# Conditioning loads issued from GpSimd's queue instead of SyncE's, in a two-layer backbone block

## The chip, the cores and the metric

The kernel runs on one core of one Trainium2 chip. The metric is the device time of one execution in microseconds, the median of several runs. Beside the times there is one profiled execution, from whose trace the rows below are read.

## What is computed

A latent stream of 256 tokens with 2048 channels goes through two layers. Layer 0 mixes tokens with a bidirectional gated recurrence and a spatial gating, layer 1 with a grouped two-dimensional Fourier transform; each mixer is followed by an MLP with a squared ReLU (2048 to 8192 to 2048). Every sublayer is wrapped in a norm, and shift, scale and gate of each norm come from a conditioning vector c through one large matrix per layer. That last part is what the change touches:

```python
for l in range(DEPTH):
    g_pre_m, g_post_m, g_pre_f, g_post_f = norm_gain[l]
    mx = [m[:, None, :] for m in jnp.split(jax.nn.silu(c) @ w_ada[l] + b_ada[l], N_MOD, axis=-1)]
    ...
    hx = modulate(x, g_pre_m, mx[0], mx[1])
    ...
    x = x + mx[2] * rmsnorm(mix_x, g_post_m)
    x = x + mx[5] * rmsnorm(sq_relu_mlp(modulate(x, g_pre_f, mx[3], mx[4]), w_mlp_in[l], w_mlp_out[l]), g_post_f)
...
def sq_relu_mlp(h, w1, w2):
    return jnp.square(jax.nn.relu(h @ w1)) @ w2
```

w_ada is 2 x 2048 x 12288 in float32, b_ada 2 x 12288. Twelve chunks of 2048 columns result, six for each layer; ten of them are "deferred" in the kernel and worked off beside the weight products.

## The kernel before

All weights stream once from HBM, as loads of [128, 2048] float32 (1 MB each, class Weights, L148) into raw tiles: two buffers `wr`, and while `spare` is set every second load goes to `ar` instead. A load holds two units of [128, 1024]. Each unit is split into a rounded high part `wh` by ScalarE (L70) and a rest `wl` by VectorE (L71), four buffers each, and TensorE makes three products of each pair (L67) instead of one. `W.get()` splits up to three units ahead of the one that TensorE is at.

The deferred conditioning (class Ada) works chunk by chunk, 16 steps a chunk. A step loads 1 MB of w_ada into one of the two `ar` buffers (L298) and adds it, times one value of silu(c), to `acc` on VectorE: the first step is a plain scaling (L301), the other 15 are multiply-adds (L307). For a gate chunk (columns 2 and 5) the first step also loads a bias row into an `ar` buffer (L304) and adds it (L305). A finished chunk is summed over the partitions by TensorE; for a gate, a row of norm gains is loaded to all partitions, also into `ar` (L351). There is one `acc` buffer, so a chunk's first step waits until the chunk before has been read.

`pump` hands out steps in the program's text: after each weight unit, 0.45 of a step in the mixer of layer 0, 0.36 in the MLP of layer 0 (which works off chunks (0,5), (1,0), (1,1), (1,3), (1,2) and begins (1,4)), 0.6 in the mixer of layer 1, 0.09 behind it; chunk (1,5) falls into the MLP of layer 1. The text's order is not the final one: the tile framework schedules the program by its own model of durations, and the instructions of each engine and each queue then stand in a fixed order and are taken in that order. What a queue's next instruction waits for holds up everything behind it on that queue.

Before the change every load, weights and conditioning, is issued by SyncE. GpSimd only prepares constants at the start.

Of the kernel before, what the change touches and what calls it, by code (L numbers as in the profile page):

```python
# [15 lines left out]
P = 128  # L16
D = 2048
KT = 16
# [18 lines left out]
def block_kernel(ctx: ExitStack, tc: tile.TileContext, a: dict, out: bass.AP, taps=None):  # L37
# [13 lines left out]

    # activations: quads of four [P, 512] slabs, and two single slabs
    def quad(dt=F32R):
# [7 lines left out]
    def slabs(n):  # L61
        """n slabs out of new quads."""
        qs = [quad() for _ in range((n + 3) // 4)]
        return [qs[i // 4][:, i % 4] for i in range(n)]
# [56 lines left out]
    class Weights:  # L121
        """Weights stream in program order: 1 MB loads, split by halves into hi + lo parts ahead of their use."""
        AHEAD = 3
# [58 lines left out]
        def place(self, u, at):  # L182
            """Unit u goes to four [P, 512] tiles: hi, hi, lo, lo."""
            assert u >= self.split_at
            self.places[u] = at
# [9 lines left out]
    class Background:  # L195
        """Latency-bound work, handed out in steps between the weight products."""

# [22 lines left out]

    # constants and small vectors
    ident = cp.tile([P, P], F32, name="ident")
# [20 lines left out]

    # silu of the conditioning vectors
    sc = cp.tile([P, 2, KT], F32, name="sc")
# [20 lines left out]
    def rstd_m2(ss, n):  # L266
        """-2 / sqrt(ss / n + eps), for the chains between sublayers."""
        s = sm.tile([P, 1], F32, name="rs")
        nc.scalar.activation(s, ss, AF.Sqrt, bias=epsb, scale=1.0 / n)
        v = sm.tile([P, 1], F32, name="rv")  # L270
        nc.vector.tensor_scalar(v, ss, 1.0 / n, EPS, ALU.mult, ALU.add)
        r = sm.tile([P, 1], F32, name="rr")
        nc.vector.reciprocal(r, s)
        e = sm.tile([P, 1], F32, name="re")
        nc.vector.scalar_tensor_tensor(e, r, r, v, ALU.mult, ALU.mult)
        r2 = sm.tile([P, 1], F32, name="rr2")
        nc.vector.scalar_tensor_tensor(r2, e, 3.0, r, ALU.subtract, ALU.mult)
        return r2

    # deferred adaLN chunks: products on VectorE, sums over partitions on TensorE  # L280
    class Ada:
# [11 lines left out]
        def step(self):  # L293
            l, c = self.order[self.pos]
            k = self.kt
            cols = slice(c * D, (c + 1) * D)
            raw = ap_.tile([P, D], F32, name="ar", tag="ar")
            nc.sync.dma_start(raw, a["w_ada"][l, k * P:(k + 1) * P, cols])  # L298
            if k == 0:
                self.acc = ap_.tile([P, D], F32, name="acc", tag="acc", bufs=1)  # L300
                self.queued(lambda: nc.vector.tensor_scalar_mul(self.acc, raw, sc[:, 0, 0:1]))  # L301
                if c in (2, 5):
                    brow = ap_.tile([P, D], F32, name="ar", tag="ar")
                    nc.sync.dma_start(brow[0:1, :], a["b_ada"][l:l + 1, cols])  # L304
                    nc.vector.tensor_add(self.acc[0:1, :], self.acc[0:1, :], brow[0:1, :])  # L305
            else:
                self.queued(lambda: nc.vector.scalar_tensor_tensor(self.acc, raw, sc[:, 0, k:k + 1], self.acc,  # L307
                                                                   ALU.mult, ALU.add))
            self.kt += 1
            if self.kt == KT:  # L310
                self.kt = 0
                self.pos += 1
                self.hold = 3
                if c in (2, 5):
                    self.done[(l, c)] = self.acc
                    if (l, c) != (0, 2):
                        self.hold = 8
                        bg.add(new_gate(l, c))
                else:
                    r = cp.tile([P, KT], F32, name=f"mod_{l}_{c}")  # L320
                    self.done[(l, c)] = r
                    bg.add(self.finish_cols(l, c, self.acc, r), front=True)
# [23 lines left out]
        def gate(self, l, c, dst):  # L346
            """-0.5 * gate * gain over all partitions (the factor meets rstd_m2)."""
            acc = self.done[(l, c)]
            gb = ap_.tile([P, D], F32, name="ar", tag="ar")
            row = l * 4 + (1 if c == 2 else 3)  # L350
            nc.sync.dma_start(gb, a["gain_rows"][row:row + 1, :].broadcast_to([P, D]))  # L351
            yield
            for b in range(4):
                t = ps()
                s = slice(b * 512, (b + 1) * 512)
                hi = rp.tile([P, 512], F32R, name="ghi", tag="xs")
                lo = rp.tile([P, 512], F32R, name="glo", tag="hh")
                split(hi, lo, acc[:, s])
                mm(t, ones_r, hi, True, False)
                mm(t, ones_r, lo, False, True)  # L360
                nc.vector.scalar_tensor_tensor(dst[:, s], t, -0.5, gb[:, s], ALU.mult, ALU.mult)
                yield
# [23 lines left out]

# [1 line left out]
    sp = tc.tile_pool(name="startp", bufs=1)  # L388
# [4 lines left out]
    def norms():  # L393
        """1 / rms of all tokens, over all partitions."""
        ss = ps()
# [18 lines left out]

    # lower bounds: softmax over the layers, first entry
    lb = cp.tile([P, 2, 8], F32, name="lb")
# [92 lines left out]
    def mm3(o, whi, wlo, h, start, stop):  # L509
        """Weights stationary: h holds hi | lo over T tokens."""  # L510
        mm(o, whi, h[:, 0:T], start, False)
        mm(o, whi, h[:, T:2 * T], False, False)
        mm(o, wlo, h[:, 0:T], False, stop)

    def tk3(o, h, t, whi, wlo, start, stop):
        """Tokens stationary: h holds hi | lo over T tokens; t picks the token tile."""
        hh = h[:, t * P:(t + 1) * P]
        hl = h[:, T + t * P:T + (t + 1) * P]
        mm(o, hh, whi, start, False)
        mm(o, hh, wlo, False, False)  # L520
        mm(o, hl, whi, False, stop)
# [39 lines left out]

# [1 line left out]
    gpool_cm = tc.tile_pool(name="gla", bufs=1)  # L563
# [9 lines left out]
    def proj_T(oL, oC, startL=True):  # L573
        """Weights stationary: one 128-column block, transposed output."""
        for half in range(2):
# [118 lines left out]
    def gla(p, st):  # L694
# [26 lines left out]

        # states left by the context
        Kt = gt("Kt", 1)
# [60 lines left out]
    def grow(Ff, Fb, KF, KB, QF, QB, B, keep):  # L784
        """Decay products over blocks of B become products over blocks of 2B."""
        n = 512 // (2 * B)
# [21 lines left out]

    # spatial gating
    vt = [[None, None], [None, None]]  # L810
# [65 lines left out]

# [1 line left out]
    rp = ctx.enter_context(tc.tile_pool(name="rp", bufs=2))  # L878
# [20 lines left out]
    def evac_product(t, nb, b, gate):  # L899
        """y <- gate * product, with the sum of squares of the product first."""  # L900
        square_sum(b, ssp[t][:, nb:nb + 1])
        yield
        nc.vector.tensor_mul(y[t][nb], gate[:, nb * 512:(nb + 1) * 512], b)
# [11 lines left out]
    def last_block(lhs, banks, start):  # L915
        """The last units of a product: the first token tile is finished before the second."""
        units = [W.get(LEAD - 1 - i) for i in range(LEAD)]
# [5 lines left out]
    def tokens_product(lhs, key, spare, upto, early=None, late=None):  # L923
        """y[t, :] = sum over KT blocks, tokens stationary."""
        gate = gates[key]
# [32 lines left out]
    def residual(evac, next_mods, consume):  # L958
        """x += gate * rmsnorm(product); next sublayer's modulated input, transposed, hi | lo.

        consume(h, t, nb) issues the next sublayer's work on token tile t, channel blocks 4 nb .. 4 nb + 3."""
        h = None
# [6 lines left out]
        def scale(parts):  # L969
            """-2 / rms of a token tile, in steps."""  # L970
            rn = sm.tile([P, 6], F32, name="rn", bufs=4)
# [107 lines left out]
    def mlp(l, ev, next_mods, rate, upto):  # L1079
# [7 lines left out]
        def start(h, t, nb):  # L1087
            """First two blocks of hidden channels, tokens stationary."""
            if t == 0 and nb == 0:
# [101 lines left out]

# [1 line left out]
    fpool_cm = tc.tile_pool(name="four", bufs=2)  # L1193
# [79 lines left out]
def _layout(inputs):  # L1273
# [51 lines left out]
    arr["w2"] = f(g["w_mlp_out"].reshape(2, 8, 2, 4, P, 4, 512).transpose(0, 1, 5, 2, 4, 3, 6)).reshape(2, 8, 4, 2, P, D)  # L1325
    # shape-only constants
    s_ = np.arange(P)[:, None]
# [32 lines left out]
```

## Time and profile before

| | us |
|---|---|
| median of three runs | 2349.06 (2347.9 to 2349.8) |
| span of the profiled execution | 2346.5 |
| TensorE busy in it | 2300.2 |
| VectorE busy | 1691.2 |
| ScalarE busy | 1164.6 |
| GpSimd busy | 0.7 |
| mean DMA rate over the span | 248 GB/s |

Matmuls are pipelined, so a busy TensorE is one that always has a product under way. A row of the view by lines gives the line of the kernel, the engine, the operation, output from input with shapes, the count, the busy time in us and the mean duration in ns, and then the idle time of the engine ahead of these instructions with what ended it. A wait is written "engine line <- what it waited for: us in total, times, longest". Stages, in us from the start of the span: startup and the first modulation up to 176, the mixer of layer 0 up to about 740, the MLP of layer 0 up to 1450, the Fourier mixer up to about 1615, the MLP of layer 1 to the end.

### The profile page before, as it was taken

How to read it: one execution, taken by the hardware profiler on the slowest of the kernel's cores; microseconds unless marked ns; L12 is line 12 of the kernel's file. 1: busy time of each engine (PE TensorE's matmuls, PEld its weight loads, DVE VectorE, ACT ScalarE, POOL GpSimd, SP SyncE). 2: the span in 40 equal slices, each digit the busy share in tenths (PEclk: the TensorE clock that was granted, in tenths of full speed). 3: DMA queues.
4: the chain of work that ended last, by engine and by line, in shares of the span. 5: the costliest groups of instructions: out<-in, count | busy, mean ns of one | idle time of the engine just before them, and what ended most of it. 6: DMA issues, size and time to landing. Idle time of an engine off the chain costs nothing.

```text
span 2346.5 us, 36060 instructions
## 1 busy us (share of the span) xinstructions
PE 2300.2 (98%) x14908; PEld 2067.8 (88%) x14908; DVE 1691.2 (72%) x1940; ACT 1164.6 (50%) x1617; POOL 0.7 (0%) x6
## 2 busy tenths in 40 slices
PE   7999999999999999999999999899999999999998
PEld 3679999998988998998998988788998998998997
DVE  7869678788556878888787787886775555556555
ACT  7766343536446554444444445646554444444443
POOL 0000000000000000000000000000000000000000
PEclk9999999999999999999999999999999999999999
DMA  8867647485564888888887897284886555555553
GB/s 342 313 248 256 225 169 293 164 302 194 193 207 150 315 321 330 326 326 336 310 324 290 316 336 290 81 312 156 305 325 216 191 184 197 180 191 204 180 195 110
DMA packets 81536, 580.92 MB, mean 248 GB/s; under 512 B 9046, under 2 KB 9046, under 8 KB 11352
## 3 DMA queue, kind: packets, MB, share of 16 engines
q1 hardware_dynamic: 81372, 578.62, 68.0%
q8 instruction: 116, 1.90, 0.3%
q14 instruction: 48, 0.39, 0.0%
HBM read 576.49 MB, written 2.10 MB: 247 GB/s over the span
## 4 chain that ended last, share of the span: by engine, by line
PE 92%; ACT 3%; DVE 3%; DMA 1%; issue 1%; SPq 0%; DVEq 0%; ACTq 0%
PE ps L67 91%; ACT wh L70 1%; DMA ar<-in_w_ada_dram 1%; ACT junk L897 1%; DMA xT<-in_xT_dram 0%; DVE wl L71 0%; ACT hh L483 0%; DVE quad L983 0%; PE ps L338 0%; PE ps L997 0%; DVE acc L307 0%; ACT quad L70 0%; ACT quad L400 0%; PE ps L614 0%; DMA wr<-in_dft_dram 0%
## 5 line engine op out<-in xcount | busy, mean ns | idle before, releaser
L70 ACT CAST wh<-wr 128x1024 fp32r<-128x1024 f32 x672 | 703.9, 1050 | 957.5 <-PE ps L67 800.4
L71 DVE TENSOR_TENSOR wl<-wr,wh 128x1024 fp32r<-128x1024 f32 x672 | 817.6, 1222 | 479.3 <-ACT wh L70 473.9
L67 PE MATMUL ps<-quad,wh 128*128 128x256 f32 x5760 | 1043.5, 284 | 3.2 <-ACT wh L70 3.2
L67 PEld LDWEIGHTS ps<-quad,wh 128*128 128x128 f32 x5760 | 898.4, 192 | 9.8 <-ACT wh L70 7.0
L67 PE MATMUL ps<-quad,wl 128*128 128x256 f32 x2880 | 811.2, 283 | 0.0
L67 PE MATMUL ps<-wh,h 128*128 128x512 f32 x1984 | 614.6, 389 | 0.0
L67 PEld LDWEIGHTS ps<-quad,wl 128*128 128x128 f32 x2880 | 551.2, 192 | 0.3 <-DVE wl L71 0.2
L67 PEld LDWEIGHTS ps<-wh,h 128*128 128x128 f32 x1984 | 372.5, 188 | 76.9
L67 PE MATMUL ps<-wl,h 128*128 128x512 f32 x992 | 386.1, 389 | 0.0
L307 DVE SCALAR_TENSOR_TENSOR acc<-ar,sc,acc 128x2048 f32<-128x2048 f32 x150 | 351.7, 2345 | 11.5 <-DMA ar<-in_w_ada_dram 10.6
L67 PE MATMUL ps<-wh,quad 128*128 128x256 f32 (+1 forms) x1248 | 322.3, 343 | 1.9 <-DVE quad L1012 1.9
L67 PEld LDWEIGHTS ps<-wh,quad 128*128 128x128 f32 x1248 | 218.5, 192 | 27.9 <-DVE quad L1012 3.5
L67 PEld LDWEIGHTS ps<-wl,h 128*128 128x128 f32 x992 | 186.3, 188 | 38.3
L67 PE MATMUL ps<-wl,quad 128*128 128x256 f32 (+1 forms) x624 | 210.9, 338 | 0.0
L67 PEld LDWEIGHTS ps<-wl,quad 128*128 128x128 f32 x624 | 120.3, 193 | 12.2 <-issue 1.0
L71 DVE TENSOR_TENSOR wl<-ar,wh 128x1024 fp32r<-128x1024 f32 x66 | 79.7, 1220 | 32.4 <-ACT wh L70 32.3
L70 ACT CAST wh<-ar 128x1024 fp32r<-128x1024 f32 x66 | 68.3, 1048 | 44.2 <-PE ps L67 41.6
L1168 DVE TENSOR_TENSOR quad<-quad,ps 128x512 f32<-128x512 f32 x96 | 62.5, 681 | 7.5 <-PE ps L67 7.5
L1137 DVE TENSOR_TENSOR h<-hh,h 128x512 fp32r<-128x512 f32 x62 | 42.8, 690 | 24.4 <-ACT h L1136 23.8
L67 PE MATMUL ps<-wl,cs 128*4 128x512 f32 x128 | 52.0, 406 | 5.3 <-DVE wl L71 4.1
L67 PE MATMUL ps<-wh,cs 128*4 128x512 f32 x128 | 52.5, 410 | 4.2 <-ACT wh L167 2.8
L1130 ACT ACTIVATE hh<-hh 128x512 f32<-128x512 f32 x62 | 39.2, 633 | 1.9
(252 smaller groups left out, 1272.5 us busy)
## 6 DMA issues: line engine op xcount, KB each, us to landing
wr<-in_w_dram SPq DMA_DIRECT2D x247, 1024.0 KB, 5.0
ar<-in_w_ada_dram SPq DMA_DIRECT2D x160, 1024.0 KB, 7.0
wr<-in_w_inT_dram SPq DMA_DIRECT2D x24, 1024.0 KB, 5.1
wr<-in_ada_s_dram SPq DMA_DIRECT2D x16, 1024.0 KB, 5.7
ar<-in_ada_s_dram SPq DMA_DIRECT2D x16, 1024.0 KB, 5.4
wr<-in_w_out_dram SPq DMA_DIRECT2D x13, 1024.0 KB, 4.8
wr<-in_w_f_dram SPq DMA_DIRECT2D x13, 1024.0 KB, 4.9
ar<-in_w_dram SPq DMA_DIRECT2D x9, 1024.0 KB, 7.2
```

What stands on the lines that cost most here:

```text
L67: nc.tensor.matmul(o, l, r, start=start, stop=stop, skip_group_check=True)
L70: nc.scalar.copy(hi, src)
L71: return nc.vector.tensor_sub(lo, src, hi.bitcast(F32))
L307: self.queued(lambda: nc.vector.scalar_tensor_tensor(self.acc, raw, sc[:, 0, k:k + 1], self.acc, ALU.mult, ALU.add))
L897: nc.scalar.activation(junk, src, AF.Square, accum_out=dst)
L1130: nc.scalar.activation(r, r, AF.Square)
L1137: nc.vector.tensor_sub(tl[:, :, 1], rv, tl[:, :, 0].bitcast(F32))
L1168: nc.vector.tensor_add(y[t][nb], y[t][nb], b[t])
```

## The change

Three loads of class Ada are issued by GpSimd's queue in place of SyncE's: the w_ada rows, the bias row and the row of norm gains. Nothing else is changed in the text; weights, tokens, small vectors and the output stay on SyncE.

```diff
@@ step
             raw = ap_.tile([P, D], F32, name="ar", tag="ar")
-            nc.sync.dma_start(raw, a["w_ada"][l, k * P:(k + 1) * P, cols])
+            nc.gpsimd.dma_start(raw, a["w_ada"][l, k * P:(k + 1) * P, cols])
...
                     brow = ap_.tile([P, D], F32, name="ar", tag="ar")
-                    nc.sync.dma_start(brow[0:1, :], a["b_ada"][l:l + 1, cols])
+                    nc.gpsimd.dma_start(brow[0:1, :], a["b_ada"][l:l + 1, cols])
@@ gate
-            nc.sync.dma_start(gb, a["gain_rows"][row:row + 1, :].broadcast_to([P, D]))
+            nc.gpsimd.dma_start(gb, a["gain_rows"][row:row + 1, :].broadcast_to([P, D]))
```

The scheduler makes another order of it. On SyncE, at the head of the MLP of layer 0, before the change (`wr` and `ar` are the raw tiles, L148 a weight load, L298 a w_ada load, L304 a bias row):

```order
L148 DMA ar<-in_w_dram 128x2048
L148 DMA wr<-in_w_dram 128x2048
L298 DMA ar<-in_w_ada_dram 128x2048
L148 DMA wr<-in_w_dram 128x2048
L304 DMA ar<-in_b_ada_dram 1x2048
L298 DMA ar<-in_w_ada_dram 128x2048 x2
```

and with it, from the same place to the Fourier matrices:

```order
L148 DMA ar<-in_w_dram 128x2048 x2
L148 DMA wr<-in_w_dram 128x2048
L148 DMA ar<-in_w_dram 128x2048
L148 DMA wr<-in_w_dram 128x2048 x122
L148 DMA wr<-in_dft_dram 128x2048
L148 DMA wr<-in_dft_dram 128x1024
```

The w_ada loads that stood between the weight loads are gone from SyncE; all 168 of them, with the bias and gain rows, now stand alone on GpSimd, in the program's order.

On VectorE, in chunk (0,5), early in the MLP of layer 0, with buffer numbers (`acc_7685` is the chunk's sum, `ar_8036` to `ar_8276` are the raw tiles of its steps 4 to 8, counted from 0), before:

```order
L71 TENSOR_TENSOR wl_8009<-wr_7982,wh_8008 128x1024
L307 SCALAR_TENSOR_TENSOR acc_7685<-ar_8036,sc_96,acc_7685 128x2048
L71 TENSOR_TENSOR wl_8040<-wr_7982,wh_8039 128x1024
L71 TENSOR_TENSOR wl_8070<-wr_8043,wh_8069 128x1024
L307 SCALAR_TENSOR_TENSOR acc_7685<-ar_8123,sc_96,acc_7685 128x2048
L71 TENSOR_TENSOR wl_8106<-wr_8043,wh_8105 128x1024
L1137 TENSOR_TENSOR h1_8100<-hh_8097,h1_8100 128x2x256
L71 TENSOR_TENSOR wl_8127<-wr_8109,wh_8126 128x1024
L307 SCALAR_TENSOR_TENSOR acc_7685<-ar_8160,sc_96,acc_7685 128x2048
```

and with the change, from the same split of `wl_8009` on:

```order
L71 TENSOR_TENSOR wl_8009<-wr_7982,wh_8008 128x1024
L307 SCALAR_TENSOR_TENSOR acc_7685<-ar_8160,sc_96,acc_7685 128x2048
L71 TENSOR_TENSOR wl_8040<-wr_7982,wh_8039 128x1024
L307 SCALAR_TENSOR_TENSOR acc_7685<-ar_8217,sc_96,acc_7685 128x2048
L71 TENSOR_TENSOR wl_8070<-wr_8043,wh_8069 128x1024
L71 TENSOR_TENSOR wl_8106<-wr_8043,wh_8105 128x1024
L307 SCALAR_TENSOR_TENSOR acc_7685<-ar_8276,sc_96,acc_7685 128x2048
L1137 TENSOR_TENSOR h1_8100<-hh_8097,h1_8100 128x2x256
L71 TENSOR_TENSOR wl_8127<-wr_8109,wh_8126 128x1024
```

The step on `ar_8160` stood four splits further on, those on `ar_8217` and `ar_8276` later still; now steps stand after one and two splits in turn, where two or three lay between them. Counted over whole chunks, the splits from a chunk's first step to its last are these, the half units at the end of a sublayer counted as halves:

| chunk | before | after |
|---|---|---|
| (0,3), (0,4), (0,2), mixer of layer 0 | 16, 12, 13 | 16, 12, 10 |
| (0,5), (1,0), (1,1), (1,3), (1,2), MLP of layer 0 | 39, 38, 38, 37, 41 | 24, 25, 22, 23, 25 |
| (1,4), half in either layer | 44 | 43 |
| (1,5), MLP of layer 1 | 39 | 24 |

The order of the 16 steps, and which buffers they use, are as before.

## Rows read from the trace of the kernel before

**Rows 1.** The page's first part: busy us, share of the span, instructions.

```profile
span 2346.5 us, 36060 instructions
...
PE 2300.2 (98%) x14908; PEld 2067.8 (88%) x14908; DVE 1691.2 (72%) x1940; ACT 1164.6 (50%) x1617; POOL 0.7 (0%) x6
```

**Rows 2.** The page's chain that ended last, shares of the span by engine.

```profile
PE 92%; ACT 3%; DVE 3%; DMA 1%; issue 1%; SPq 0%; DVEq 0%; ACTq 0%
```

**Rows 3.** Busy time by stretches; last: granted clock, DMA share, GB/s.

```profile
core 0: us, PE busy (x) PEld busy (x) DVE busy (x) ACT busy (x) POOL busy (x), PEclk, DMA share, GB/s
5.00:30.00 25.00, 16.39 (x42) 4.99 (x42) 18.57 (x26) 21.79 (x26) 0.00 (x0) 0.99 1.01 422
176.00:610.00 434.00, 432.19 (x3350) 416.75 (x3348) 353.31 (x530) 202.70 (x334) 0.00 (x0) 1.00 0.63 226
756.00:1450.00 694.00, 694.00 (x4469) 635.78 (x4469) 559.30 (x457) 322.91 (x365) 0.00 (x0) 1.00 0.86 320
1450.00:1500.00 50.00, 42.31 (x200) 34.76 (x199) 39.79 (x96) 32.48 (x90) 0.00 (x0) 0.90 0.25 94
1640.00:1770.00 130.00, 130.00 (x896) 121.65 (x895) 97.77 (x72) 67.22 (x80) 0.00 (x0) 1.00 0.86 315
```

**Rows 4.** Timeline of ScalarE in the MLP: start, us, instruction, idle before it.

```profile
915.89 1.06 ACT L70 CAST wh<-wr 128x1024 fp32r<-128x1024 f32 x1 [1.67 <-PE ps L67]
918.61 1.05 ACT L70 CAST wh<-wr 128x1024 fp32r<-128x1024 f32 x1 [1.66 <-PE ps L67]
...
937.85 1.05 ACT L70 CAST wh<-wr 128x1024 fp32r<-128x1024 f32 x1 [1.83 <-PE ps L67]
940.73 1.05 ACT L70 CAST wh<-wr 128x1024 fp32r<-128x1024 f32 x1 [1.83 <-PE ps L67]
```

**Rows 5.** The view by lines: split of a unit, and conditioning steps.

```profile
L71 DVE TENSOR_TENSOR wl<-wr,wh 128x1024 fp32r<-128x1024 f32 x672 | 817.6, 1222 | 479.3 <-ACT wh L70 473.9 <-PE ps L67 4.7
L70 ACT CAST wh<-wr 128x1024 fp32r<-128x1024 f32 x672 | 703.9, 1050 | 957.5 <-PE ps L67 800.4 <-DMA wr<-in_w_dram 124.6 <-DMA wr<-in_w_f_dram 12.8
L307 DVE SCALAR_TENSOR_TENSOR acc<-ar,sc,acc 128x2048 f32<-128x2048 f32 x150 | 351.7, 2345 | 11.5 <-DMA ar<-in_w_ada_dram 10.6 <-DVE wl L71 0.2
...
L301 DVE TENSOR_SCALAR acc<-ar,sc 128x2048 f32<-128x2048 f32 x10 | 12.8, 1280 | 0.3 <-DMA ar<-in_w_ada_dram 0.3
```

**Rows 6.** Timeline of SyncE's queue in the MLP of layer 0.

```profile
913.36 0.33 SPq L148 DMA_DIRECT2D wr<-in_w_dram  x1
913.74 0.42 SPq L298 DMA_DIRECT2D ar<-in_w_ada_dram  x1
```

**Rows 7.** Loads issued from 756 to 1450 us; last: median us to landing.

```profile
wr<-in_w_dram SPq DMA_DIRECT2D x121, 1024.0 KB, 5.0
ar<-in_w_ada_dram SPq DMA_DIRECT2D x88, 1024.0 KB, 7.1
```

**Rows 8.** The chain in the mixer of layer 0: start, us, what.

```profile
394.98 2.26 DVE acc L307
...
397.27 4.62 DMA ar<-in_w_ada_dram
...
507.02 5.53 DMA ar<-in_w_ada_dram
```

**Rows 9.** Waits from 756 to 1440 us.

```profile
ACT wh L70 <- DMA wr<-in_w_dram: 97.4, 40, 5.2
...
DVE acc L307 <- DMA ar<-in_w_ada_dram: 1.9, 8, 0.4
```

**Rows 10.** Waits of SyncE's queue, whole span.

```profile
SPq L298 <- DVE acc L307: 99.5, 34, 8.0
```

**Rows 11.** Timeline of VectorE at the end of layer 0.

```profile
1433.62 2.34 DVE L307 SCALAR_TENSOR_TENSOR acc<-ar,sc,acc 128x2048 f32<-128x2048 f32 x1
1435.88 1.28 DVE L909 TENSOR_TENSOR quad<-quad,gate 128x512 f32<-128x512 f32 x2
1437.08 3.64 DVE L71 TENSOR_TENSOR wl<-wr,wh 128x1024 fp32r<-128x1024 f32 x3
```

**Rows 12.** The chain there.

```profile
1455.28 2.50 DVE quad L71 x4
1457.80 3.48 DMA wr<-in_dft_dram
```

## Prediction

> **What bounds the kernel now.** I read the page's first part first: TensorE is busy 2300.2 of 2346.5 us, VectorE 1691.2, GpSimd 0.7 [rows 1]. Then the chain that ended last: 92% of it is TensorE, 1% a DMA [rows 2]. So a transfer can only give time back where TensorE stands idle, and those places are few. The table by stages shows them [rows 3]: in the layer 0 mixer (176 to 610 us) TensorE is idle 1.8 us, in the MLP of layer 0 (756 to 1450) not at all, at the start of the MLP of layer 1 (1640 to 1770) not at all, and at the seam between the layers (1450 to 1500) 7.7 us. The rest of its 46 us lies in startup and in the other seams, where no conditioning load is due. The gain that this change could reach is therefore under 10 us.
>
> What it could cost is read from the same table: in the MLP of layer 0 VectorE is busy 559.3 of 694 us and the DMA engines 86% at 320 GB/s, while the most that the trace shows them moving is 422 GB/s, at startup. TensorE is the bound there, with two engines close behind it.
>
> How close, from three further views. The pace: ScalarE starts a weight unit's cast whenever TensorE frees a buffer, every 2.72 us in the down product and 2.88 us in the up product [rows 4]; both halves are equally long, so 2.80 us a unit. The cushion: there are four wh and four wl tiles, so a unit's split may begin three units before TensorE needs it, 8.4 us; the split itself takes 1.05 + 1.22 us [rows 5]; 6.1 us are left before a late split stops TensorE. The work of a unit on VectorE: 1.22 us for the split, and 2.35 us for each conditioning product [rows 5].
>
> **The change part by part.** *The issues.* 168 loads (160 of w_ada, 4 bias rows, 4 norm rows) leave SyncE and go to GpSimd, which had 0.7 us of work. On SyncE an issue holds the queue 0.33 to 0.42 us [rows 6]; nobody waits for that in the MLP, so it is worth nothing. What SyncE's queue loses is the blocking: it no longer stops at a w_ada load whose buffer is taken. In the MLP that buys nothing either, since TensorE never waits there: 40 weight loads already come late for ScalarE, 97.4 us in sum [rows 9], and the cushion swallows all of it.
>
> *The order on VectorE.* This is the real change, and it is seen in the built order, not in the diff. On SyncE's queue a w_ada load stood between the weight loads, and the products stood evenly, one in 2.6 units. On a queue of its own the load runs ahead of the program, and the scheduler puts the products wherever it finds room: a chunk's products now stand 1.6 units apart, and then none for some twenty units. Six chunks lie wholly in an MLP; between first and last product they had 39, 38, 38, 37, 41 and 39 splits and now have 24, 25, 22, 23, 25 and 24. The order binds: a product whose load is late now stands in front of splits that TensorE needs.
>
> *What the DMA engines must deliver in such a burst.* In 24 units, 67 us at TensorE's pace, 12 loads of weights and 14 of w_ada (two are there before it starts), 26 times 1.049 MB: 407 GB/s. Startup reached 422, the MLP runs at 320 [rows 3]. It is near what the trace shows to be possible at all.
>
> *What the two ar buffers allow.* The load of product k+2 can be issued when product k has ended. Call L the time from that end to the start of product k+2. Product 0 is a plain scaling of 1.28 us, product 1 takes 2.35 us [rows 5] and ends at 3.6 us at the earliest; product 15 follows seven loads and six products later: 3.6 + 7 L + 6 x 2.35 = 17.7 + 7 L. In three of the six chunks (the first, fifth and sixth) a bias row holds the second buffer at the head, so product 1 has to wait for a load of its own; it meets little traffic, and I take the 5.53 us of [rows 8] for it: 23.2 + 7 L. The schedule gives product 15 its number of units times 2.80, and the cushion another 6.1 us: 73.3, 76.1, 67.7, 70.5, 76.1 and 73.3 us. What is over goes to TensorE, chunk by chunk.
>
> *L.* No row shows a load issued by GpSimd, and none shows this crowd, so it is bounded. Alone, right after a product, a w_ada load came in 4.62 us, in light traffic in 5.53 us [rows 8]. Issued just behind a weight load [rows 6] its median is 7.1 us, the weight load's own 5.0 [rows 7]: one transfer ahead costs 2.5 us. In a burst the engines are nearly always busy, so one transfer ahead is the usual case, and at times the other ar load is ahead too; I add a quarter of a transfer for that: 4.6 + 2.5 + 0.6 = 7.7 us. GpSimd's issue I count like SyncE's, since nothing else is in its queue. The low bound is 5.5 us (light traffic), the high one 9.5 us (today's 7.1 and a whole product of 2.35 us for which the issue is held up); 7.7 lies nearest to the 7.1 because that row is the only one with weights beside it. At L = 7.7 product 15 begins at 71.6 us, or 77.1 with a bias row; over are 3.8, 0, 3.9, 1.1, 1.0 and 3.8, together 13.6 us.
>
> The Trainium skill has a price for the queue itself: DMA: Bandwidth & Descriptors, section "Anatomy of one DMA — SWDGE (gpsimd) path", fits a GpSimd load as about 2.0 us plus its bytes at 436 GB/s, by which 1 MiB takes 4.4 us (an estimate from that page), no more than SyncE's 4.62 us. With that for the lone load the sum would be about 7 us instead of 14; no row here shows a GpSimd load yet.
>
> *The rest.* In the mixer the DMA engines are at 63% [rows 3], and its three chunks keep nearly their spacing (16, 12 and 13 splits become 16, 12 and 10); I count 0 with 2 us either way. The chunk that straddles the seam has 7 products before it, three turns, inside the cushion. The sum is made on the profiled execution: 2346.5 + 13.6 = 2360.1 us; the median of the runs lies 2.6 us above the span, so 2363 us.
>
> **The rivals.** *The cushion holds.* At L = 7.4 only 5 us are over in all six chunks, about what a measurement of this kernel can tell from no change (0.2%, 4.7 us); at 7.1, today's median, nothing is over. For it: VectorE waits only 1.9 us for w_ada in the whole stage now [rows 9], and a load that no longer stands behind a weight load in one queue may come sooner. Against it: the 407 GB/s asked of the engines. It gives 2347 to 2354, say 2350 us.
>
> *Faster, through the seam.* At the end of layer 0 a product stands on VectorE at 1433.62, in front of three splits [rows 11]; the last weight buffers come free late, the second transform matrix arrives only after a wait of 3.48 us, and ScalarE and the norm chain on VectorE, which stands behind its split, wait for it [rows 12]. After the change that product stands some nine units earlier, and SyncE's queue, which waited 99.5 us for conditioning products over the whole kernel [rows 10], reaches the matrices without them. Then 3.5 to 7.7 us of TensorE's idle time could go. This decides only if the bursts cost nothing (L below 7.1) and more than 4.7 us come back: 2343 us. Against it: the matrix waits for a buffer that a weight split frees, not for the queue.
>
> *VectorE holds GpSimd up.* If an issue on GpSimd had to wait for the running VectorE instruction, up to 2.35 us would be added to L. At L = 9.5 the six chunks lose 16.4, 8.1, 16.5, 13.7, 13.6 and 16.4 us, together 85 us: 2434 us. VectorE is 81% busy in that stage [rows 3], so it would strike most loads. For or against it the trace of before says nothing; only that of after can.
>
> The Trainium skill states such a lock, but a narrower one: SBUF — State Buffer, sections "SBUF: two separate sides" and "Who interferes with whom", says that GpSimd cannot write descriptors while VectorE runs an operation in a mode that takes both ports, and that tensor_tensor has no such mode. By its speed only the plain scaling (2048 columns in 1280 ns, ten times) looks like that mode here, the products (2345 ns) do not; by the page this rival would be small, which is why its chance is. No run here shows it yet.
>
> *The change does not act:* the same spacing on the chip as before. The built order already differs, so this has no chance beyond that of the first rival.
>
> **How the numbers follow.** Bursts that overrun the cushion (L from 7.4 to 8.7): 0.45, the likeliest, 2363 us. The cushion holds: 0.35. VectorE holds GpSimd up, or L is above 8.7 for another reason: 0.11. Faster through the seam: 0.09. Slower by over 0.2% is the first and third, 0.56; within 0.2% 0.35; faster 0.09. The range leaves out most of the faster case and of the third: its low end, 2345, is the held cushion with a part of the seam; its high end, 2400, is L = 8.7 (51 us over).
>
> **What will show it.** Right: in the MLP of layer 0 VectorE waits for ar many times longer than 1.9 us, TensorE waits for wl in the last third of a chunk's products, DMA share swings between the high nineties and half, and TensorE has 10 to 50 us of idle time in that stage. The tightest chunk, 22 units, loses most. Wrong: TensorE without idle time there, which means that L stayed under 7.1 us; or idle time outside the bursts, which means that weight loads, not w_ada, became late; or a VectorE product or split that itself got longer, a contention that I have not priced.

## The result: 2434 us, 3.6% slower

The changed kernel takes 2433.94 us (median of four runs, 2430.3 to 2434.7) where the kernel before takes 2348.48 beside it: a ratio of 1.036, 95% interval 1.0346 to 1.0374. The forecast was 2363 us, range 2345 to 2400. The sign was right, the size was not: 85 us are lost where 14 were counted.

The page of the changed kernel, its first part and its chain, against [rows 1, 2]:

```profile
span 2432.4 us, 36195 instructions
...
PE 2330.8 (96%) x14908; PEld 2078.1 (85%) x14908; DVE 1689.9 (69%) x1940; ACT 1155.2 (47%) x1617; POOL 89.5 (4%) x174
...
PE 63%; DMA 15%; DVE 10%; issue 8%; ACT 4%; POOL 0%; SPq 0%; DVEq 0%; ACTq 0%; POOLq 0%
```

The span grew by 85.9 us. TensorE is idle 101.6 us instead of 46.3, and busy 30.6 us longer for the same 14908 products. The chain, 92% TensorE before, is now 15% DMA and 10% VectorE: the program waits for data.

Where, by stretches (columns as in [rows 3]): first the MLP of layer 0, then the burst of chunk (0,5), the quiet stretch behind it, and the bursts of (1,0), (1,3) and (1,2).

```profile
756.00:1450.00 694.00, 661.89 (x4169) 595.73 (x4168) 518.25 (x424) 291.45 (x337) 45.41 (x86) 0.99 0.79 295
769.00:853.00 84.00, 78.37 (x479) 67.92 (x477) 68.87 (x46) 35.01 (x44) 8.96 (x17) 1.00 0.91 342
853.00:903.00 50.00, 48.92 (x383) 47.83 (x384) 29.19 (x29) 27.39 (x34) 0.53 (x1) 1.00 0.63 223
903.00:984.00 81.00, 78.12 (x475) 70.05 (x474) 71.88 (x54) 31.57 (x35) 8.45 (x16) 1.00 0.96 363
1169.00:1249.00 80.00, 75.04 (x426) 64.51 (x426) 67.46 (x50) 29.44 (x34) 7.93 (x15) 0.98 0.91 348
1307.00:1397.00 90.00, 81.37 (x515) 74.21 (x514) 72.27 (x52) 30.13 (x35) 8.47 (x16) 0.96 0.84 322
```

The even 0.86 of before has become 0.91 to 0.96 in three of these bursts and 0.63 behind the first. Chunk (1,2), which lost most, is the exception: 0.84 in the mean, at 322 GB/s, no more than the stage moved before. TensorE is idle 32.1 us in this stage, where it never was.

The landings in the first burst, in the quiet stretch, and those of the weights in the bursts of (1,0) and (1,2) (columns as in [rows 7]):

```profile
ar<-in_w_ada_dram POOLq DMA_DIRECT2D x15, 1024.0 KB, 7.2
wr<-in_w_dram SPq DMA_DIRECT2D x11, 1024.0 KB, 7.8
...
wr<-in_w_dram SPq DMA_DIRECT2D x10, 1024.0 KB, 5.0
...
wr<-in_w_dram SPq DMA_DIRECT2D x13, 1024.0 KB, 6.9
...
wr<-in_w_dram SPq DMA_DIRECT2D x13, 1024.0 KB, 8.4
```

The w_ada load takes the 7.2 us it took before (7.1). The weight load is what suffers: 6.9 to 8.4 us in the bursts, 5.0 out of them, 5.0 before. The waits from 756 to 1450 us, against [rows 9]:

```profile
POOL ar L298 <- DVE acc L307: 310.8, 67, 10.7
ACT wh L70 <- DMA wr<-in_w_dram: 270.7, 73, 9.5
...
PEld ps L67 <- DVE wl L71: 35.7, 32, 2.8
DVE acc L307 <- DMA ar<-in_w_ada_dram: 35.1, 28, 4.7
PE ps L67 <- DVE wl L71: 25.2, 29, 2.5
```

ScalarE's wait for weights went from 97.4 to 270.7 us, VectorE's for w_ada from 1.9 to 35.1. ScalarE's timeline in the first burst (columns as in [rows 4]) shows what that looks like: the casts no longer come singly as TensorE frees a buffer, but in pairs, when a load has landed.

```profile
795.91 2.00 ACT L70 CAST wh<-wr 128x1024 fp32r<-128x1024 f32 x2 [5.62 <-DMA wr<-in_w_dram]
801.64 2.00 ACT L70 CAST wh<-wr 128x1024 fp32r<-128x1024 f32 x2 [1.93 <-DMA wr<-in_w_dram]
807.25 2.00 ACT L70 CAST wh<-wr 128x1024 fp32r<-128x1024 f32 x2 [3.61 <-DMA wr<-in_w_dram]
...
836.39 1.05 ACT L70 CAST wh<-wr 128x1024 fp32r<-128x1024 f32 x1 [7.11 <-DMA wr<-in_w_dram]
```

The chain inside that burst (start, us, what):

```profile
777.60 7.00 DMA ar<-in_w_ada_dram
...
788.20 7.61 DMA wr<-in_w_dram
...
802.02 7.08 DMA ar<-in_w_ada_dram
...
811.84 8.99 DMA ar<-in_w_ada_dram
...
823.57 7.56 DMA ar<-in_w_ada_dram
...
833.87 5.32 DMA ar<-in_w_ada_dram
...
841.92 8.52 DMA ar<-in_w_ada_dram
```

Both loops are in it: six w_ada loads and, between the first two, one weight load.

VectorE and GpSimd, by lines:

```profile
L71 DVE TENSOR_TENSOR wl<-wr,wh 128x1024 fp32r<-128x1024 f32 x672 | 815.2, 1222 | 516.0 <-ACT wh L70 513.3 <-PE ps L67 2.1
L307 DVE SCALAR_TENSOR_TENSOR acc<-ar,sc,acc 128x2048 f32<-128x2048 f32 x150 | 352.0, 2347 | 71.9 <-DMA ar<-in_w_ada_dram 71.5
L298 POOL DMA_DIRECT2D ar<-in_w_ada_dram x160 | 84.7, 529 | 1665.1 <-DVE acc L307 594.6 <-DVE wl L71 511.5 <-DVE acc L301 328.1
```

No instruction of VectorE got longer (1222 and 2347 ns; before 1222 and 2345), and a GpSimd issue takes 0.53 us in the mean.

The loss, stage by stage, read from one and the same split (L71) in the two timelines of VectorE, what the prediction counted, and the median time to landing of the burst's weight loads. A split further on or back moves a row by 1 to 2 us.

| | predicted | measured | weight load lands in |
|---|---|---|---|
| mixer of layer 0 | 0 | 10.0 | |
| chunk (0,5) and the quiet stretch behind it | 3.8 | 9.4 | 7.8 |
| (1,0) | 0 | 5.4 | 6.9 |
| (1,1) | 3.9 | 9.9 | 7.5 |
| (1,3) | 1.1 | 8.3 | 7.3 |
| (1,2) | 1.0 | 17.1 | 8.4 |
| (1,4), over the seam and the Fourier mixer | 0 | 11.5 | |
| (1,5), MLP of layer 1 | 3.8 | 14.8 | 8.2 |

The loss of a burst goes with the landing of its weights: the two bursts at 8.2 and 8.4 us lost most, the one at 6.9 least. The w_ada loads land in 6.9 to 7.4 us in all six.

### The profile page after: what moved, and what is told of

Same layout as the page of the kernel before. It is cut to its first block, busy times and chain, and to the rows that moved or that the text cites. A ratio compares the mean times of both kernels' runs of the same rounds, so it can differ in the third digit from the quotient of the medians.

```text
span 2432.4 us, 36195 instructions
## 1 busy us (share of the span) xinstructions
PE 2330.8 (96%) x14908; PEld 2078.1 (85%) x14908; DVE 1689.9 (69%) x1940; ACT 1155.2 (47%) x1617; POOL 89.5 (4%) x174
## 4 chain that ended last, share of the span: by engine, by line
PE 63%; DMA 15%; DVE 10%; issue 8%; ACT 4%; POOL 0%; SPq 0%; DVEq 0%; ACTq 0%; POOLq 0%
PE ps L67 62%; DMA ar<-in_w_ada_dram 7%; DMA wr<-in_w_dram 7%; DVE wl L71 4%; DVE acc L307 3%; ACT wh L70 2%; DMA wr<-in_w_f_dram 1%; ACT junk L897 1%; DMA xT<-in_xT_dram 0%; DVE quad L983 0%; ACT hh L483 0%; PE ps L338 0%; PE ps L997 0%; ACT quad L70 0%; DVE quad L906 0%
## 5 line engine op out<-in xcount | busy, mean ns | idle before, releaser
L70 ACT CAST wh<-wr 128x1024 fp32r<-128x1024 f32 x672 | 695.5, 1049 | 1066.0 <-PE ps L67 677.3
L71 DVE TENSOR_TENSOR wl<-wr,wh 128x1024 fp32r<-128x1024 f32 x672 | 815.2, 1222 | 516.0 <-ACT wh L70 513.3
L67 PE MATMUL ps<-quad,wl 128*128 128x256 f32 x2880 | 815.6, 285 | 13.2 <-DVE wl L71 13.1
L67 PE MATMUL ps<-wl,h 128*128 128x512 f32 x992 | 391.4, 395 | 20.2 <-DVE wl L71 20.1
L307 DVE SCALAR_TENSOR_TENSOR acc<-ar,sc,acc 128x2048 f32<-128x2048 f32 x150 | 352.0, 2347 | 71.9 <-DMA ar<-in_w_ada_dram 71.5
L298 POOL DMA_DIRECT2D ar<-in_w_ada_dram x160 | 84.7, 529 | 1665.1 <-DVE acc L307 594.6
L71 DVE TENSOR_TENSOR wl<-ar,wh 128x1024 fp32r<-128x1024 f32 x66 | 79.7, 1220 | 32.7 <-ACT wh L70 32.5
```

Source lines behind the costliest of these rows:

```text
L67: nc.tensor.matmul(o, l, r, start=start, stop=stop, skip_group_check=True)
L70: nc.scalar.copy(hi, src)
L71: return nc.vector.tensor_sub(lo, src, hi.bitcast(F32))
L298: nc.gpsimd.dma_start(raw, a["w_ada"][l, k * P:(k + 1) * P, cols])
```

## The experiments

### Order or queue: four kernels

The change does two things: another queue, and, through the scheduler, another order on VectorE. To part them, products from chunk (0,5) on were tied behind the split they follow in the text. The mixer was left to the scheduler.

```diff
         def queued(self, op):
-            if self.behind is None:
+            if self.behind is None and self.pos >= 3:
+                with tc.issue_after(W.last.ins):
+                    op()
+            elif self.behind is None:
                 op()
...
-R4 = 0.09
+R4 = 0.36
```

That gives the even order. For the bursts, against the even order:

```diff
-R2 = 0.36
-R4 = 0.36
+R2 = 0.64
+R4 = 0.64
...
-            self.credit += rate
             if self.hold:
                 self.hold -= 1
+                self.credit += rate if self.pos < 3 else 0.0
                 return
+            self.credit += rate
...
-                self.hold = 3
+                self.hold = 3 if self.pos < 4 else 20
...
-                        self.hold = 8
+                        self.hold = 8 if self.pos < 4 else 20
```

Each was built from the kernel before (SyncE) and from the changed one (GpSimd).

> GpSimd issues the conditioning loads, as in the changed kernel, but from chunk (0,5) on each product is tied behind the split it follows in the program's text, so that a chunk's products stand 36 to 41 splits apart from first to last, as in the kernel before (the chunk over the seam 33). If the order on VectorE is what costs (my prediction's mechanism): within 5 us of the kernel before behind the mixer, 2349 to 2358 in all (the mixer's 9 us may stay, its order is that of the changed kernel). If the queue itself costs (GpSimd's issue, its ring beside SyncE's): still near 2434. Waits for conditioning loads on VectorE under 10 us by the first, near 70 by the second.

> SyncE issues all loads, as in the kernel before, but the products are handed out in bursts: a chunk's products span 22 to 25 splits from chunk (0,5) on (the seam chunk 36), then none for about twenty. If the order costs whatever the queue: 2400 to 2440, with the loss in the six bursts, 7 to 17 us each. If bursts cost only with a second queue: 2345 to 2355. The mixer is as before (no loss there under either).

> The same bursts handed out by the text, on GpSimd's queue: 23 or 24 splits for a chunk, the changed kernel's order but for single places. It is the partner of the bursts on SyncE. Both theories: 2425 to 2440, as the changed kernel. If it is far below, then it is not the bursts as such but what else the scheduler moved.

> SyncE issues all loads and the products are tied to the text at the pace of the kernel before (37 to 41 splits a chunk): the partner of the even order on GpSimd. Both theories: 2345 to 2355, as the kernel before. If it is slower, then tying products to the text costs by itself, and the run on GpSimd is to be read against this one.

Measured, medians in us and ratio to the kernel before, with its interval:

| | even (33 to 41 splits a chunk) | bursts (22 to 25) |
|---|---|---|
| SyncE | 2365.3, 1.0067 [1.005, 1.0083] | 2438.0, 1.0373 [1.0358, 1.0389] |
| GpSimd | 2384.1, 1.0143 [1.0127, 1.016] | 2467.6, 1.0497 [1.0465, 1.0529] |

The order costs 73 us on SyncE and 84 on GpSimd; the queue 19 us at the even order and 30 in bursts. Of the 19 us about 12 lie in the mixer, where the products were not tied and the two orders differ. So the order is the main thing, and **it costs whatever the queue**: bursts on SyncE, with not one instruction on GpSimd more than before, are as slow as the changed kernel. My even expectations were missed: tying products to the text costs 15 us by itself on SyncE (late in chunk (1,2) and at the seam), and GpSimd's queue adds to that. The bursts on GpSimd came out 28 us above what I expected.

The same order does not lose in the same way on both queues. Chunk (1,3) of the bursts on SyncE, by stretch and by waits, those of SyncE's queue last (columns as in [rows 10]):

```profile
1175.00:1256.00 81.00, 67.88 (x388) 58.91 (x386) 71.10 (x52) 30.62 (x34) 0.00 (x0) 0.96 0.90 345
```

```profile
ACT wh L70 <- DMA wr<-in_w_dram: 39.5, 10, 6.9
...
DVE acc L307 <- DMA ar<-in_w_ada_dram: 0.4, 2, 0.2
...
SPq L298 <- DVE acc L307: 31.0, 11, 6.6
```

VectorE waits 0.4 us for w_ada, and TensorE is idle 13.1 us all the same, behind 39.5 us of waits for weights. The ar loop still has a part in it: SyncE's queue stands 31.0 us at w_ada loads whose buffer a product still reads, and the weight loads behind them stand too. In the kernel before, no load of this chunk waited for a multiply-add (1130 to 1240 us). On two queues no weight load stands behind a w_ada load, and there both kinds are waited for (VectorE waits 7.2 us for w_ada in the changed kernel's burst of the same chunk). So the two burst kernels show that this order is slow on either queue; how much of each loss goes which way they do not show. The even order on SyncE stands at w_ada loads as well, 163.4 us at 53 of them from 756 to 1450 us where the kernel before stands 8.0 us at three; that is a likely reason for its 15 us, not a tested one.

### Bytes or VectorE's time: three kernels and the changed one

In a burst two things run short: the DMA engines (a share of 0.84 to 0.96) and VectorE, which has 65.8 to 72.3 us of work in bursts of 22 to 25 units, 62 to 70 us at TensorE's pace. The bursts on GpSimd were run with half of each w_ada load (the products' other operands are folded to match):

```diff
-            nc.gpsimd.dma_start(raw, a["w_ada"][l, k * P:(k + 1) * P, cols])
+            nc.gpsimd.dma_start(raw[:, 0:D // 2], a["w_ada"][l, k * P:(k + 1) * P, c * D:c * D + D // 2])
+            raw = raw[:, None, 0:D // 2].broadcast_to([P, 2, D // 2])
```

with products on 512 of the 2048 columns (W8 is 512):

```diff
-                self.queued(lambda: nc.vector.scalar_tensor_tensor(self.acc, raw, sc[:, 0, k:k + 1], self.acc,
+                self.queued(lambda: nc.vector.scalar_tensor_tensor(self.acc[:, 0:W8], raw[:, 0:W8], sc[:, 0, k:k + 1], self.acc[:, 0:W8],
```

and with both; and the changed kernel itself with half of each load.

> The bursts handed out by the text on GpSimd's queue (2467.5), with half of each conditioning load left out: 512 KB come instead of 1 MB, and a product reads that half twice, so VectorE's work and order in the four chunks (1,0) to (1,2) are the same. In those four chunks the kernel it is made from loses 55 us against the kernel before. If the bytes are what is short (DMA engines at a share of 0.91 to 0.96 in a burst): under 12 us remain there, DMA share in the bursts near 0.7, weight loads land in 5.0 to 5.5 us, in all 2360 to 2400. If VectorE's time is what is short (65.7 to 72.3 us of work in 62 to 70 us of TensorE's pace): 40 us or more remain there, in all above 2430.

> The same bursts with whole loads, but each product after a chunk's first covers 512 of 2048 columns (the rest of the multiply-adds is left out): about 0.6 us instead of 2.35 on VectorE, the bytes and the order in the chunks (1,0) to (1,2) the same. If the bytes are short: 40 us or more of the 55 remain in those chunks, DMA share in the bursts at 0.9 and more, in all above 2420. If VectorE is short: under 12 us remain there, in all 2360 to 2400. If both together make it (either relieved is enough): little remains in this run and in the one with half the bytes.

> The bursts on GpSimd's queue with both reliefs: half of each conditioning load left out, and products after a chunk's first on 512 of 2048 columns (the rest of the multiply-adds left out). With half the bytes alone 24 us of the 55 remained in the chunks (1,0) to (1,2), with short products alone 41. If bytes and VectorE's time are the two causes and nothing else: under 6 us remain there, in all 2350 to 2375. If a third cause stands behind them (the second ring, the two wr buffers, the order itself): 15 us or more remain.

> The changed kernel itself with half of each conditioning load left out (a product reads the half twice; order in the MLP of layer 0 as in the changed kernel, 22 to 25 splits a chunk; 2434 with whole loads). If the bytes carry most of the changed kernel's 85 us: 50 to 65 us go, 2370 to 2385, what VectorE's time alone costs stays. If the hand-made bursts misled about the changed kernel: 2410 or more.

| | us, ratio | lost in the chunks (1,0) to (1,2) |
|---|---|---|
| bursts on GpSimd | 2467.6 | 56.9 |
| half the bytes | 2399.2, 1.0205 [1.0182, 1.0228] | 23.3 |
| short products | 2438.1, 1.037 [1.0346, 1.0394] | 43.7 |
| both | 2379.5, 1.0125 [1.0109, 1.0142] | 6.9 |
| changed kernel | 2433.9, 1.036 | 39.4 |
| changed kernel, half the bytes | 2361.6, 1.0057 [1.0042, 1.0072] | 3.4 |

The last column is read between two splits into wl, those that start at 889.29 and 1393.83 us in the kernel before and that stand behind the first step of (1,0) and of (1,4). Other splits near them give up to 5 us more or less (the 55, 24 and 41 of the expectations come from such splits), and a kernel that takes the same time as before (the last one below) reads 4.9, so differences below 5 us say nothing here.

Chunk (1,3) in the three kernels; half the bytes:

```profile
1160.00:1232.00 72.00, 67.44 (x390) 59.58 (x390) 67.44 (x49) 31.03 (x34) 8.08 (x16) 0.98 0.80 284
```

short products:

```profile
1179.00:1260.00 81.00, 69.97 (x396) 60.18 (x396) 45.49 (x51) 30.35 (x34) 8.42 (x16) 0.99 0.91 346
```

both:

```profile
1159.00:1228.00 69.00, 69.00 (x408) 61.46 (x407) 46.37 (x52) 31.18 (x34) 8.43 (x16) 1.00 0.83 298
```

With half the bytes the chunk takes 72 us and VectorE is busy 67.4 of them: now it is the limit. With short products VectorE has 35 us to spare, and the chunk still takes 81, at a DMA share of 0.91. With both, 69 us, and TensorE is never idle. My expectation for half the bytes (under 12 us left, a share near 0.7) was missed, with twice the loss and a share of 0.80: there are **two limits, the nearer one the bytes**. The changed kernel says the same more clearly: half the bytes give back 72 of its 85 us, with the same spacing on VectorE in the MLP, more than the 50 to 65 I expected; the median landing of its weights in chunk (1,3) goes from 7.3 us to 6.3. A third cause beside the two is not needed in these chunks (6.9 us with both, just above the 6 I named). In all, the kernel with both missed its 2350 to 2375: 16 us of its loss lie in the mixer, where short products make another order (12, 7 and 6 splits a chunk).

Half a load is also sooner landed. So these runs do not part a limit of the DMA engines from a limit of the loops, in which a load has only two buffers to go to. A third buffer, which would part them, was not tried.

### From which pace on

> GpSimd's queue with products tied to the text at a pace between the even one and the bursts: 32 splits a chunk in the chunks (1,0) to (1,2), where even has 36 to 41 and the bursts 23. The engines are asked for 30 loads in 32 x 2.80 us, 351 GB/s, and moved up to 375 in the bursts; VectorE has about 79 us of work in 89.6. If there is a ceiling: nothing is short yet, 2380 to 2390, as the even order on GpSimd (2384), under 8 us lost in those four chunks. If the loss grows evenly with the pace: half way to the bursts, 2415 to 2435.

The edit, against the bursts on GpSimd:

```diff
-R2 = 0.64
-R4 = 0.64
+R2 = 0.47
+R4 = 0.47
...
-                self.hold = 3 if self.pos < 4 else 20
+                self.hold = 3 if self.pos < 4 else 12
...
-                        self.hold = 8 if self.pos < 4 else 20
+                        self.hold = 8 if self.pos < 4 else 12
```

Measured: 2441.7 us, 1.0401 [1.0384, 1.0418], above both expectations. In the chunks (1,0) to (1,2) it loses 33.5 us, 8.4 a chunk, against 14.2 in the bursts; the even order on GpSimd loses 10.5 in all there, 2.6 a chunk. Asked for are 351 GB/s, 407 in the bursts and about 320 at the even order. Chunk (1,3) at this pace:

```profile
1185.00:1284.00 99.00, 94.91 (x611) 86.37 (x609) 80.38 (x61) 39.62 (x44) 7.93 (x15) 1.00 0.87 323
```

It moves 323 GB/s at a share of 0.87, hardly more than the stage before the change (320 at 0.86), and still loses. So **there is no threshold at which the engines are full**: the loss sets in below that and grows with the pace. The rest of this kernel's time went in the mixer, in chunk (0,5), at the seam and in (1,5), where its order differs too; I did not part those.

### The queue by itself

In the mixer the order on GpSimd differed a little from that on SyncE (10 splits instead of 13 in chunk (0,2)). Two kernels have every product tied to the text, the mixer's too, so that both have the same spacing (single splits aside). Against the even order:

```diff
-            if self.behind is None and self.pos >= 3:
+            if self.behind is None:
                 with tc.issue_after(W.last.ins):
                     op()
-            elif self.behind is None:
-                op()
```

> As the even order on GpSimd (2384), with the products of the mixer tied to the text too (26, 20 and 19 splits for its three chunks instead of 16, 12 and 10). The 12.3 us that the even order on GpSimd lost in the mixer: if the order there made them, they go, 2365 to 2373 in all; if the queue made them (a load on GpSimd's queue that waits or lands longer), they stay, 2380 or more.

> The same order of products on SyncE's queue, the partner of the run before: 2360 to 2368, as the even order on SyncE. The difference of the two is what the queue itself costs at one and the same order on VectorE: under 5 us if the order is nearly all, 10 to 20 us if GpSimd's queue has a price of its own.

GpSimd 2380.6 us (2376.2 to 2383.9), 1.0138 [1.0121, 1.0154]; SyncE 2370.8 (2366.7 to 2373.7), 1.009 [1.0075, 1.0105], above what I expected for it. So by the medians 10 us belong to the queue at the same order, at the edge of what the second theory said. The mixer lost about 10 us on GpSimd and 9 on SyncE: tying its products costs by itself nearly what it was to save, so the 12 us are not explained by this pair, and at the same spacing the queue makes little there. The two profiled runs lie only 2.5 us apart (spans of 2374.4 and 2371.9 us), so the traces cannot place the 10 us of the medians. Landings from 880 to 1400 us, on GpSimd:

```profile
wr<-in_w_dram SPq DMA_DIRECT2D x91, 1024.0 KB, 6.2
ar<-in_w_ada_dram POOLq DMA_DIRECT2D x65, 1024.0 KB, 5.2
```

and on SyncE:

```profile
wr<-in_w_dram SPq DMA_DIRECT2D x90, 1024.0 KB, 6.5
ar<-in_w_ada_dram SPq DMA_DIRECT2D x64, 1024.0 KB, 6.9
```

A w_ada load lands 1.7 us sooner from its own queue, and weights no later. So neither landing explains the 10 us; what does stays open.

### One part alone

> The other part of the change alone: only the four bias rows and the four norm rows on GpSimd's queue, w_ada stays on SyncE; the products span 36 to 41 splits a chunk in the MLP of layer 0, as before. If the w_ada loads carry the whole effect: 2344 to 2356, no difference that counts; 8 loads less on SyncE might give a microsecond or two. If a GpSimd load in the middle of the stream disturbs by itself (its landing, its ring): over 2360.

```diff
-                    nc.sync.dma_start(brow[0:1, :], a["b_ada"][l:l + 1, cols])
+                    nc.gpsimd.dma_start(brow[0:1, :], a["b_ada"][l:l + 1, cols])
...
-            nc.sync.dma_start(gb, a["gain_rows"][row:row + 1, :].broadcast_to([P, D]))
+            nc.gpsimd.dma_start(gb, a["gain_rows"][row:row + 1, :].broadcast_to([P, D]))
```

2350.5 us, 1.0011 [1.0001, 1.002]: no difference that counts. The 160 w_ada loads carry the whole effect. None of the twelve kernels beats the one before.

## Why the prediction was wrong by size

**What bounds the kernel: right.** TensorE, with the DMA engines and VectorE close behind; nothing was to be gained in the MLP, and nothing was. The seam gave nothing back either: (1,4) across it lost 11.5 us.

**The issues, worth nothing: right.** GpSimd takes 0.53 us an issue, 0.1 to 0.2 us more than SyncE, with no row of VectorE that pays for it.

**The order on VectorE: right.** The bursts are there, and they cost as much on SyncE's queue. This was the step that carried the sign.

**The delivery: the step that failed.** The prediction worked out 407 GB/s for a burst, called it near the 422 of startup, and then gave the crowd a price only in the w_ada loads. Two things were wrong. The mean demand of a burst was compared with the peak of a short stretch: the engines do reach 428 GB/s for 10 us of a burst (see *Full, then empty* below), but over whole bursts they moved 322 to 363. And the delay was shared: the weight loads went from 5.0 to 6.9 to 8.4 us and ScalarE's wait for them to 270.7 us. The prediction worked out the loop of the two ar buffers and not that of the two wr buffers. A load of weights holds two units, so at 2.80 us a unit a wr buffer comes round every 11.2 us; two casts (2.00 us) and the last split (1.22 us) take 3.2 of them, and about 8.0 us are left for the load, an estimate from these rows. The medians of the bursts come near that or pass it, and the loss goes with them. In the text that stood only as a sign of being wrong ("weight loads, not w_ada, became late"), with no price and no rival. The Trainium skill has the rule in DMA: Bandwidth & Descriptors, section "Issuing engines are not separate DMA queues": loads started by different engines end up on the same 16 engines and interleave there. The trace agrees: with the second queue filled it is the weights, whose own queue was cleared, that land later (7.8 us for 5.0 in the first burst).

**L and the head of a chunk: near, and too short.** Six w_ada loads of the chain in chunk (0,5) take 7.41 us in the mean, with 0.28 us ahead of each: 7.7 us, the value chosen. As the prediction defines it, from a product's end to the start of the next but one, L along products 1, 3, to 15 is 7.8, 7.8, 8.0, 8.6, 9.2 and 8.1 us in the six chunks. The head of chunk (0,5), its product 1 and its product 15 on VectorE (columns as in [rows 11]):

```profile
769.22 1.29 DVE L301 TENSOR_SCALAR acc<-ar,sc 128x2048 f32<-128x2048 f32 x1 [0.78 <-DMA ar<-in_w_ada_dram]
...
775.02 2.27 DVE L305 TENSOR_TENSOR acc<-acc,ar 1x2048 f32<-1x2048 f32 x1
...
779.50 2.34 DVE L307 SCALAR_TENSOR_TENSOR acc<-ar,sc,acc 128x2048 f32<-128x2048 f32 x1
...
850.54 2.35 DVE L307 SCALAR_TENSOR_TENSOR acc<-ar,sc,acc 128x2048 f32<-128x2048 f32 x1 [1.94 <-DMA ar<-in_w_ada_dram]
```

Product 1 ended 12.6 us after the chunk's start, where 9.1 were counted; the adding of the bias row, 2.27 us, was in no term. Product 15 was due at 77.1 us and began at 81.3. In the other five it began at 78.8, 73.9, 78.1, 87.7 and 84.6 us, where the sum has 71.6, 71.6, 71.6, 77.1 and 77.1.

**The cushion: the second failure.** The sum let each chunk use up 6.1 us before TensorE pays. With the measured starts of product 15 its rule gives 8.0, 2.7, 6.2, 7.6, 11.6 and 11.3 us, together 47 where 65 were lost in the six chunks; and product 15 is late in part because it stands behind splits that wait for weights, so this sum does not part the two loops. The splits that were to fill the cushion wait for the weights, and those were late themselves; and VectorE, with up to 72.3 us of work in a burst, was short of time too, the second limit, which with half the bytes still cost 23.3 us in four chunks of the hand-made bursts (3.4 in the changed kernel). The loss does not go by a chunk's units either, as the prediction's sign said it would: (1,1), the tightest with 22, lost 9.9 us, (1,2) with 25 lost 17.1.

**The mixer and the seam, counted at 0 with 2 us: wrong.** 10.0 and 11.5 us. In the mixer VectorE waits for ar as the prediction's loop says, 21.2 us from 176 to 756 us where it waited 7.1 before; with half the bytes about 4 us are left of the 10.

**The rivals.** The held cushion fell with 85 us; the seam gave nothing. *VectorE holds GpSimd up* named 2434 us, the time measured, for a reason that is not there: issues take 0.53 us in the mean, in the chain of the first burst the next one follows a product's end within 0.28 us, and bursts on SyncE are as slow. The Trainium skill (SBUF — State Buffer, "Who interferes with whom") says that tensor_tensor has no mode that takes both ports. The trace agrees for the splits, which are tensor_tensor and take 1222 ns as before; for the products, which are scalar_tensor_tensor, the rows alone speak (2347 ns for 2345).

Its other signs read right: 32 us of idle TensorE in the stage (10 to 50 forecast), waits for wl, a swinging DMA share. The sign for late weights, idle time outside the bursts, stayed away, and yet they were late: inside the bursts (TensorE is idle 1.1 us from 853 to 903). The signs did not tell a loss of 14 us from one of 85.

## What to carry to other kernels

A transfer that goes to another queue shares the same engines, so look for its price in the loads that stay: do not take the peak of a short stretch for what a whole burst can have, and ask what the longer landing does to every loop of buffers, not only to that of the loads that move. Where a scheduler sets the order, moving an issue moves the work behind it; compare the built orders, and count bytes and VectorE's time per burst, since the order of the kernel before asked 320 GB/s evenly and left TensorE no idle time, while bursts of the same work cost 70 us and more than an even order on the same queue. An average below the peak is no cover with two buffers a loop: with 351 GB/s asked, where 428 are reached for a while, each chunk already lost 8.4 us.

## What the runs showed of the hardware

**A short wait can cost twice.** In chunk (1,2) of the changed kernel TensorE stood between waits from 1356.5 to 1360 us; the stretches of one microsecond (columns as in [rows 3]):

```profile
1359.00:1360.00 1.00, 0.00 (x0) 0.00 (x0) 0.98 (x1) 0.94 (x3) 0.53 (x1) 1.00 0.08 33
1360.00:1361.00 1.00, 0.97 (x8) 0.97 (x9) 0.00 (x0) 0.49 (x1) 0.00 (x0) 1.00 0.76 164
...
1362.00:1363.00 1.00, 1.00 (x7) 1.00 (x6) 1.00 (x1) 1.00 (x2) 0.00 (x0) 0.50 1.02 434
1363.00:1364.00 1.00, 1.00 (x6) 1.00 (x6) 1.00 (x2) 0.67 (x1) 0.00 (x0) 0.50 0.38 156
...
1366.00:1367.00 1.00, 1.00 (x11) 1.00 (x10) 1.00 (x2) 0.00 (x0) 0.00 (x0) 1.00 0.78 311
```

TensorE worked again from 1360 on, and then the granted clock fell to 0.50, the lower of its two levels (1.2 GHz), for some three microseconds; it makes 6 or 7 products in a microsecond instead of 11. Not every wait had this: TensorE stood 2.55 us from 974.8 us on, and the granted clock stayed at 1.00 (973 to 985 us). The mean clock over the span is 0.986 against 0.992. That is about 30 us more at the half clock (0.014 x 2432 / 0.5, less 0.008 x 2347 / 0.5), an estimate of 15 us of the loss, and part of the 30.6 us that TensorE is busy longer. The prediction had no term for it.

**Full, then empty.** The same rows show the DMA engines at a share of 0.08 at 1359 and at 1.02 at 1362. There are two buffers for each of the two kinds, so at most four of these loads can be in the air, and at 1359 none of them moves much. Ten microseconds of the burst of (1,0):

```profile
937.00:947.00 10.00, 10.00 (x46) 8.29 (x45) 8.79 (x9) 2.79 (x3) 1.05 (x2) 1.00 1.02 428
```

So the engines can be full at 428 GB/s in the middle of a burst, while whole bursts move 322 to 363. That the few buffers are why the mean stays there is argued from these rows; no kernel with more buffers was run.

**Startup.** In seven of the twelve kernels the granted clock is lower at the start, in work that is the same in all. The first 60 us of the kernel before, and of the tied order on SyncE:

```profile
0.00:60.00 60.00, 44.29 (x190) 19.90 (x191) 47.23 (x69) 45.10 (x58) 0.70 (x6) 0.97 0.90 345
```

```profile
0.00:60.00 60.00, 45.12 (x188) 20.68 (x189) 46.54 (x68) 44.37 (x56) 0.70 (x6) 0.94 0.89 339
```

The granted clock there is 0.91 to 0.94 instead of 0.97 (by these means, 7 to 11 us of the first 60 at the half clock instead of 4). It costs little: the first w_ada load is issued at 155.2 to 156.6 us in these seven, at 154.7 in the kernel before. No comparison above hangs on it. Its cause is open.
